# Modulation products on a 32-column stationary block spread over the four column quarters of TensorE

## The chip, the cores and the metric

The kernel runs on one core of a Trainium2 chip. The metric is the device time of one execution in microseconds (us); the median of three runs is given. In the profile PE is TensorE's matmul, PEld its weight load, DVE VectorE, ACT ScalarE, POOL GpSimd, SP the engine that issues most DMAs.

## What is computed

Two layers of a block with attention, retention and state-space heads and an MLP, all in float32. Ahead of both sub-layers of a layer stands a modulation, which is what the change touches:

```python
sc = jax.nn.silu(c); scc = jax.nn.silu(c_ctx)          # two vectors of 1024
mod   = sc  @ w_mod[layer] + b_mod[layer]              # [1024] @ [1024, 6144]
mod_c = scc @ w_mod[layer] + b_mod[layer]              # the same for the context stream
sh1, sc1, g1, sh2, sc2, g2 = jnp.split(mod, 6, axis=-1)
h  = rmsnorm(x, norm_g[0]) * (1 + sc1) + sh1           # ahead of the mixers
x  = x + g1 * rmsnorm(o, norm_g[1])                    # behind them
```

So each layer has two vector-by-matrix products with a matrix of 1024 x 6144, which is 25 MB a layer in float32.

## The kernel before

The 6144 columns are worked in 12 sections of 512 columns (`sec`), the 1024 rows in 8 chunks of 128 (`k`). For a section on TensorE the stationary operand is `csil[:, k, :]`, 128 rows by 2 columns (the two streams), the moving operand is a chunk of weights, 128x512, and the output is a tile `mq` of 2x512 in PSUM, summed over the chunks. ACT copies it to SBUF as `mr`; four transposes turn it into columns, one feature to a partition (`mps`), DVE adds the bias (`mc`) and writes the table `abc` from which the norm is modulated.

The 12 sections of layer 0 are made in three places. At the program's start, in `start`, sections 0, 2 and 3 are made by `mod_exact` on TensorE, with weights in tiles `m`, and section 1 by `mod_sums`, in which DVE multiplies and adds eight chunks for two streams into `acc_m` and TensorE only sums over the partitions (L369). Woven into them are the transposes of the normed input (`xps`) and their copies back to SBUF. The first weights of the mixers, `kv`, are converted there too (`wr_kv` to `wh_kv` and `wl_kv`). The next norm needs sections 0 and 2 for its first four chunks, and sections 1 and 3 for the others; then come the `kvp` products. In the mixers of layer 0, sections 4 to 9 are a list of steps (`mods_gen`) that runs in the gaps of attention and retention. Sections 4 and 5 go through `mod_split`: ACT rounds the raw weights `wr_m` to a high part `wh_m`, POOL subtracts for the low part `wl_m`, and `chl`, four columns of high and low parts of `csil`, is multiplied with either. Sections 6 to 9 go through `mod_whole`: float32 products straight from `wr_m`. Sections 10, 11 and all of layer 1 are made later by `mod_groups`, outside the change.

All raw weights in the mixers share the tag `wr` with three buffers of 128x1024, so a load waits until the buffer three loads earlier has been read. Nearly all DMAs are issued by SP, in order. The order on each engine comes from a scheduler that keeps the program's order as priority and moves instructions by its own estimates, so an edit in one place reorders its neighbours. Instructions on one engine run in that order. Behind section 9 follow the retention heads 1 to 3 (`dTkr`, `dTqr`, `rs`, `rd`, the state `rst`, the output `ry`), then the output projection (`op`).

Of the kernel before, what the change touches and what calls it, by code (L numbers as in the profile page):

```python
# [20 lines left out]
D = 1024  # L21
# [21 lines left out]
def shape_constants():  # L43
# [16 lines left out]
    # query minus key in a chunk; steps from the chunk before to a query, for both directions  # L60
# [20 lines left out]
def tile_hybrid_backbone(  # L81
# [87 lines left out]
    def rsqrt_mean(y, ssum, use, D=D, n=1):  # L169
        """1 / sqrt(ssum / D + EPS): the scalar engine's root, then one Newton step on its reciprocal"""  # L170
# [12 lines left out]
    def softplus(y, xin, n):  # L183
        """log(1 + exp(x)) = max(x, 0) + 2 atanh(e / (2 + e)), e = exp(-|x|)"""
# [17 lines left out]
    def wraw(src, shape, name):  # L202
        """one half of a unit: at most 1024 elements a partition"""
        r = wp.tile([128, 1024], F32, tag="wr", name=f"wr_{name}", bufs=3)
        v = r[:, : shape[1] * shape[2]].rearrange("p (a b) -> p a b", a=shape[1])
        for s_ap, c0, n0 in src:
            nc.sync.dma_start(v[:, :, c0 : c0 + n0], s_ap)
        return v

    def wunit(src, shape, name, lo_eng=None, pool=None):  # L210
        """src: function (first row block, row blocks) -> list of (AP, first column, columns)"""
# [13 lines left out]
    def wcols(w, k0, cols):  # L225
        """row blocks from k0 on; cols: list of (column in w, column in the unit, columns)"""
# [18 lines left out]
    chl = cp.tile([128, KC, 4], F32R, name="chl")  # L245
    V.tensor_copy(chl[:, :, 0:4:2], csil)
    V.tensor_tensor(chl[:, :, 1:4:2], csil, chl[:, :, 0:4:2].bitcast(F32), ALU.subtract)

    # gate * norm gain: [mixer or channel, stream]
    grow = [dp.tile([2, 2, D], F32, name=f"grow{l}") for l in range(DEPTH)]  # L250
    pcol = [cp.tile([128, R_END], F32, name=f"pcol{l}") for l in range(DEPTH)]
    # per layer: A1, B1, A2, B2, each [chunk, stream]
# [18 lines left out]
    def mod_cols(l, sec, q, nrow):  # L271
        """section of 512 columns of the modulation, as per-feature columns; q: [nrow, 512] in SBUF"""
        which = sec // 2
        k0 = 4 * (sec % 2)
        if q.shape[0] == 128:
            o = q
        else:
            o = pC([128, 4, nrow], f"mps{l}_{sec}")
            for k in range(4):
                transpose(o[:, k, :], q[:, k * 128 : (k + 1) * 128])  # L280
# [4 lines left out]
        if nrow == 2:  # L285
            V.tensor_tensor(tk, o, bcol, ALU.add)
        else:
            u = sm.tile([128, 4, 4], F32, tag="mc_u", name=f"mu{l}_{sec}")
            S.activation(u, o, AF.Copy)
            V.tensor_tensor(tk, u[:, :, 0:4:2], u[:, :, 1:4:2], ALU.add)  # L290
            V.tensor_tensor(tk, tk, bcol, ALU.add)
# [28 lines left out]
    def mod_whole(l, sec, row):  # L320
        q = pB([2, 512], f"mq{l}_{sec}")
        for u in range(4):
            r = wraw(wcols(w_mod[l], 0, [(sec * 512, 0, 512)])(2 * u, 2), (128, 2, 512), f"m{l}_{sec}_{u}")
            for k in range(2):
                T.matmul(q, csil[:, 2 * u + k, :], r[:, k], start=u + k == 0, stop=u + k == 4)
            if u == 3:
                r = row([2, 512], f"mr{l}_{sec}")
# [4 lines left out]
    def mod_split(l, sec, row):  # L332
        q = pB([4, 512], f"mq{l}_{sec}")
        for u in range(4):
            if u % 2 == 0:
                hu, lu = wunit(wcols(w_mod[l], 2 * u, [(sec * 512, 0, 512)]), (128, 4, 512), f"m{l}_{sec}_{u}", G)
            h, lo = hu[:, 2 * (u % 2) : 2 * (u % 2) + 2], lu[:, 2 * (u % 2) : 2 * (u % 2) + 2]
            for k in range(2):
                for w in (h, lo):
# [1134 lines left out]
```

## Time and profile before

| what | value |
|---|---|
| median of 3 runs | 1888.09 us (1886.2 to 1888.5) |
| span of the profiled execution | 1880.8 us |
| median less that span | 7.3 us |
| PE busy | 1753.1 us, 93% |
| DVE, ACT, POOL busy | 1219.7, 703.0, 369.1 us |
| granted TensorE clock, mean | 0.972 |

The profile gives the span from the first to the last instruction; its execution has no other time of its own, and the runs beside it take 7.3 us more than the span. A float32 matmul stands in the trace as two records of PE, each with a weight load of its own; one of the rounded type stands as one record. PE records overlap, since a record lasts until its last result is written: what a record costs in a row of them is the distance between starts.

### The profile page before, as it was taken

What the parts mean: (1) busy time and instruction counts of PE and PEld (TensorE: products, weight loads), DVE (VectorE), ACT (ScalarE), POOL (GpSimd) and SP (SyncE); (2) the same over time, 40 slices, a digit from 0 to 9 for tenths busy, and PEclk for the clock granted to TensorE, in tenths of its full rate; (3) what the DMA queues carried; (4) which work ended last, traced back from release to release, by engine and by line L of the source; (5) the groups of instructions that cost most, each with busy time, mean ns of one, the idle gap of its engine ahead of it and who ended that gap; (6) DMA issues with size and microseconds to landing.
All of it is one profiled execution on the core that took longest, in us unless ns stands there. A gap on an engine that the chain in (4) does not pass through costs nothing. (4 is left out here: it accounts for less than half of the span.)

```text
span 1880.8 us, 24641 instructions
## 1 busy us (share of the span) xinstructions
PE 1753.1 (93%) x8991; PEld 1443.0 (77%) x8991; DVE 1219.7 (65%) x2462; ACT 703.0 (37%) x1267; POOL 369.1 (20%) x391
## 2 busy tenths in 40 slices
PE   6987999997999999999999979888987999999998
PEld 2877977655878888888888868777866788888886
DVE  5868985664668566566566586788876654444445
ACT  5543376652461111201201275433772532222222
POOL 0047232313001100100100132553022021111112
PEclk9999999997999999999999999999996999999999
DMA  8410243366444334434434433224324432222332
GB/s 274 124 52 32 89 149 104 104 182 184 146 135 136 124 101 132 125 107 123 126 105 118 152 123 91 65 71 124 100 73 110 147 122 90 90 90 91 102 105 95
DMA packets 189078, 217.00 MB, mean 115 GB/s; under 512 B 67667, under 2 KB 142237, under 8 KB 188957
## 3 DMA queue, kind: packets, MB, share of 16 engines
q1 hardware_dynamic: 188956, 215.43, 37.8%
q8 instruction: 71, 1.16, 0.2%
q14 instruction: 51, 0.41, 0.1%
HBM read 189.66 MB, written 25.72 MB: 115 GB/s over the span
## 5 line engine op out<-in xcount | busy, mean ns | idle before, releaser
L467 PE MATMUL f<-h_h,wh_f 128*128 128x512 f32 (+1 forms) x800 | 280.3, 351 | 1.4 <-ACT h_h L448 1.4
L469 PE MATMUL f<-h_h,wl_f 128*128 128x512 f32 (+1 forms) x800 | 281.0, 352 | 0.0
L468 PE MATMUL f<-h_l,wh_f 128*128 128x512 f32 (+1 forms) x800 | 280.1, 350 | 0.8 <-DVE h_l L449 0.8
L1299 POOL TENSOR_TENSOR r<-r 128x768 f32<-128x768 f32 (+1 forms) x64 | 93.8, 1466 | 847.4 <-ACT r L1298 837.8
L467 PE MATMUL f<-wh_g,uh 128*128 128x512 f32 x640 | 253.0, 396 | 4.1 <-DVE acc L1327 1.7
L468 PE MATMUL f<-wl_g,uh 128*128 128x512 f32 x640 | 252.6, 395 | 0.0
L469 PE MATMUL f<-wh_g,ul 128*128 128x512 f32 x640 | 251.8, 394 | 0.0
L221 ACT ACTIVATE wh_f<-wr_f 128x1024 fp32r<-128x1024 f32 x64 | 66.5, 1055 | 377.2 <-PE f L469 164.4
L1329 DVE TENSOR_TENSOR acc<-acc,f 128x512 f32<-128x512 f32 x140 | 96.0, 686 | 121.0 <-PE f L469 119.6
L467 PEld LDWEIGHTS f<-h_h,wh_f 128*128 128x128 f32 x800 | 152.0, 190 | 23.0 <-ACT h_h L448 1.5
L468 PEld LDWEIGHTS f<-h_l,wh_f 128*128 128x128 f32 x800 | 151.1, 189 | 22.8 <-DVE h_l L449 1.0
L469 PEld LDWEIGHTS f<-h_h,wl_f 128*128 128x128 f32 x800 | 151.2, 189 | 20.8
L405 DVE SCALAR_TENSOR_TENSOR ga<-wr_mg,cg_a,ga 128x512 f32<-128x512 f32 x216 | 153.6, 762 | 14.6 <-DMA wr_mg<-in_w_mod_dram 14.6
L467 PEld LDWEIGHTS f<-wh_g,uh 128*128 128x128 f32 x640 | 120.1, 188 | 33.5 <-DVE acc L1327 2.2
L469 PEld LDWEIGHTS f<-wh_g,ul 128*128 128x128 f32 x640 | 120.1, 188 | 28.8
L468 PEld LDWEIGHTS f<-wl_g,uh 128*128 128x128 f32 x640 | 120.2, 188 | 27.4 <-DVE wl_g L222 0.2
L1298 ACT ACTIVATE r<-f 128x768 f32<-128x768 f32 (+1 forms) x64 | 44.8, 699 | 193.4 <-PE f L469 133.4
L1300 DVE CAST uh<-r 128x768 fp32r<-128x768 f32 (+1 forms) x64 | 32.3, 505 | 123.2 <-POOL r L1299 123.2
L222 DVE TENSOR_TENSOR wl_f<-wr_f,wh_f 128x1024 fp32r<-128x1024 f32 x64 | 77.6, 1220 | 51.3 <-ACT wh_f L221 51.3
L222 DVE TENSOR_TENSOR wl_g<-wr_g,wh_g 128x1024 fp32r<-128x1024 f32 x62 | 76.6, 1241 | 50.9 <-ACT wh_g L221 50.8
L221 ACT ACTIVATE wh_g<-wr_g 128x1024 fp32r<-128x1024 f32 x64 | 67.3, 1056 | 94.2 <-DMA wr_g<-in_w_ff_dram 53.6
L467 PE MATMUL xbc<-h_h,wh_xbc 128*128 128x512 f32 (+1 forms) x208 | 73.5, 353 | 7.7 <-ACT cin L692 7.7
(405 smaller groups left out, 3774.3 us busy)
## 6 DMA issues: line engine op xcount, KB each, us to landing
wr_f<-in_w_ff_dram SPq DMA_DIRECT2D x64, 512.0 KB, 3.7
wr_g<-in_w_ff_dram SPq DMA_DIRECT2D x64, 512.0 KB, 3.5
wr_mg<-in_w_mod_dram SPq DMA_DIRECT2D x192, 128.0 KB, 2.9
wr_m<-in_w_mod_dram SPq DMA_DIRECT2D x24, 512.0 KB, 3.8
m<-in_w_mod_dram SPq DMA_DIRECT2D x32, 256.0 KB, 4.2
wr_o<-in_w_out_dram SPq DMA_DIRECT2D x16, 512.0 KB, 4.1
wr_xbc<-in_w_in_dram SPq DMA_DIRECT2D x14, 512.0 KB, 5.3
xmid<-xt SPq DMA_DIRECT2D x10, 512.0 KB, 2.6
```

Of the source, the lines that this page charges most:

```text
L221: S.activation(hv[:, a0 : a0 + an], r, AF.Copy)
L222: (lo_eng or V).tensor_tensor(lv[:, a0 : a0 + an], r, hv[:, a0 : a0 + an].bitcast(F32), ALU.subtract)
L405: V.scalar_tensor_tensor(acc[:, s], r2[:, k % 2], w, acc[:, s], ALU.mult, ALU.add)
L467: T.matmul(o, a[0], b[0], start=first, stop=False)
L468: T.matmul(o, a[0], b[1], start=False, stop=False)
L469: T.matmul(o, a[1], b[0], start=False, stop=last)
L1298: S.activation(r, q[:, :NT], AF.Relu)
L1299: G.tensor_tensor(r, r, r, ALU.mult)
L1300: V.tensor_copy(uh, r)
L1329: V.tensor_tensor(acc[tt][:, ns], acc[tt][:, ns], qs[tt][half], ALU.add)
```

## The change

The stationary operand becomes `cwide[:, k, :]`: the two columns of `csil` and 30 columns of zeros. Chunk `k` writes to partitions 32 (k mod 4) to 32 (k mod 4) + 31 of a 128x512 tile `mq`, so two chunks share each quarter and successive chunks go to different quarters. The built program has a column position of 0, 32, 64 or 96 at these matmuls, and a tile of 128x32 both before and after. The four partial sums are added in the step that made the four transposes: `mr` (now 128x512) is the stationary operand of four float32 matmuls with `qsum`, 128x2, whose ones sit where a row's number modulo 32 is the stream's. `mod_split` is gone: sections 4 and 5 go through `mod_whole`. `mod_sums`, with `csil`, stays. The parts of the diff that are left out drop comments.

```diff
-    chl = cp.tile([128, KC, 4], F32R, name="chl")
-    V.tensor_copy(chl[:, :, 0:4:2], csil)
-    V.tensor_tensor(chl[:, :, 1:4:2], csil, chl[:, :, 0:4:2].bitcast(F32), ALU.subtract)
+    cwide = cp.tile([128, KC, 32], F32, name="cwide")
+    G.memset(cwide, 0.0)
+    G.tensor_copy(cwide[:, :, 0:2], csil)
+    qsum = cp.tile([128, 2], F32, name="qsum")
+    V.tensor_reduce(qsum, ident.rearrange("p (j r) -> p r j", r=32)[:, 0:2, :], AX.X, ALU.add)
...
     def mod_cols(l, sec, q, nrow):
-        if q.shape[0] == 128:
+        if len(q.shape) == 3:
             o = q
         else:
             o = pC([128, 4, nrow], f"mps{l}_{sec}")
             for k in range(4):
-                transpose(o[:, k, :], q[:, k * 128 : (k + 1) * 128])
+                T.matmul(o[:, k, :], q[:, k * 128 : (k + 1) * 128], qsum, start=True, stop=True)
...
+    def mod_quarter(q, k, v):
+        j = k % 4
+        T.matmul(q[32 * j : 32 * j + 32], cwide[:, k, :], v, start=k < 4, stop=k >= KC - 4)
+
     def mod_exact(l, sec, raw, row):
-        q = pB([2, 512], f"mq{l}_{sec}")
+        q = pB([128, 512], f"mq{l}_{sec}")
         for k in range(KC):
...
-            T.matmul(q, csil[:, k, :], v, start=k == 0, stop=k == KC - 1)
+            mod_quarter(q, k, v)
...
     def mod_whole(l, sec, row):
-        q = pB([2, 512], f"mq{l}_{sec}")
+        q = pB([128, 512], f"mq{l}_{sec}")
...
             for k in range(2):
-                T.matmul(q, csil[:, 2 * u + k, :], r[:, k], start=u + k == 0, stop=u + k == 4)
+                mod_quarter(q, 2 * u + k, r[:, k])
...
-    def mod_split(l, sec, row):
...
-                    yield from (mod_whole if s in (6,7,8,9,) else mod_split)(0, s, lambda shape, name: mp.tile([128, 512], F32, tag="fcol", name=name)[: shape[0]])
+                    yield from mod_whole(0, s, lambda shape, name: mp.tile([128, 512], F32, tag="fcol", name=name)[: shape[0]])
```

The scheduler's order moves with it. In the start stage DVE had these rows before; names read as tile, section, chunk and buffer, so `acc_m<-m_1_0` is the first chunk of section 1:

```order
L269 TENSOR_SCALAR pcol_104<-pcol_104 128x42
L361 TENSOR_SCALAR acc_m<-m_1_0_225,csil 128x512 x2
L286 TENSOR_TENSOR mc_0_218<-mps_0_213,pcol_104 128x4x2
L295 COPY abc_106<-mc_0_218 128x8
L1411 COPY x_120<-xps_200 128x512
L363 SCALAR_TENSOR_TENSOR acc_m<-m_1_1_232,csil,acc_m 128x512 x2
L363 SCALAR_TENSOR_TENSOR acc_m<-m_1_2_250,csil,acc_m 128x512 x2
```

And now:

```order
L273 TENSOR_SCALAR pcol_106<-pcol_106 128x42
L1398 COPY x_122<-xps_202 128x512
L289 TENSOR_TENSOR mc_0_220<-mps_0_215,pcol_106 128x4x2
L348 TENSOR_SCALAR acc_m<-m_1_0_227,csil 128x512
L293 COPY abc_108<-mc_0_220 128x8
L348 TENSOR_SCALAR acc_m<-m_1_0_227,csil 128x512
L1398 COPY x_122<-xps_238 128x512
L350 SCALAR_TENSOR_TENSOR acc_m<-m_1_1_234,csil,acc_m 128x512 x2
```

The first sums of section 1 now stand behind `mc_0`, which needs the end of section 0, and one copy of `xps` stands ahead of both. On PE, at the same place, the products of section 0 stood together before:

```order
L152 MATMUL pps_178<-ident,prow_172 128x125
L314 MATMUL mq_0_165<-m_0_2_182,csil 2x512
L314 MATMUL mq_0_165<-m_0_3_185,csil 2x512
L314 MATMUL mq_0_165<-m_0_4_188,csil 2x512
L314 MATMUL mq_0_165<-m_0_5_191,csil 2x512
L314 MATMUL mq_0_165<-m_0_6_194,csil 2x512
L314 MATMUL mq_0_165<-m_0_7_197,csil 2x512
L152 MATMUL xps_200<-ident,x_120 128x128 x8
L152 MATMUL mps_0_213<-ident,mr_0_211 128x2 x4
L314 MATMUL mq_2_221<-m_2_0_222,csil 2x512
```

Now sixteen transposes `xps` stand between them:

```order
L152 MATMUL xps_202<-ident,x_122 128x128 x6
L310 MATMUL mq_0_167<-m_0_2_184,cwide 32x512
L152 MATMUL xps_202<-ident,x_122 128x128 x2
L152 MATMUL xps_238<-ident,x_122 128x128 x3
L310 MATMUL mq_0_167<-m_0_3_187,cwide 32x512
L152 MATMUL xps_238<-ident,x_122 128x128 x5
L310 MATMUL mq_0_167<-m_0_4_190,cwide 32x512
L310 MATMUL mq_0_167<-m_0_5_193,cwide 32x512
L310 MATMUL mq_0_167<-m_0_6_196,cwide 32x512
L310 MATMUL mq_0_167<-m_0_7_199,cwide 32x512
L310 MATMUL mq_2_223<-m_2_0_224,cwide 32x512
L284 MATMUL mps_0_215<-qsum,mr_0_213 128x2 x4
```

The last six chunks of section 0 are no longer one block, and the sum over quarters, `mps_0`, comes behind the first chunk of section 2.

In attention PE had, at the seam of sections 4 and 5, pairs of products with a high and a low part between score products `s` and transposes `pt`:

```order
L340 MATMUL mq_4_3652<-wh_m_4_2_3774,chl 4x512
L340 MATMUL mq_4_3652<-wl_m_4_2_3775,chl 4x512
L340 MATMUL mq_5_3948<-wh_m_5_0_3949,chl 4x512
L340 MATMUL mq_5_3948<-wl_m_5_0_3950,chl 4x512
L152 MATMUL pt_3600<-ident,P_3595 128x128 x3
L152 MATMUL pt_3606<-ident,P_3595 128x128 x3
L938 MATMUL s_3692<-k1a_2958,qha_3293 128x512
L939 MATMUL s_3692<-k1a_2958,qla_3294 128x512
L938 MATMUL s_3692<-k1a_2958,qha_3293 128x256
L939 MATMUL s_3692<-k1a_2958,qla_3294 128x256
L340 MATMUL mq_5_3948<-wh_m_5_0_3949,chl 4x512
L340 MATMUL mq_5_3948<-wl_m_5_0_3950,chl 4x512
```

There stands now this, in which `x2` is two chunks of one buffer:

```order
L310 MATMUL mq_4_3654<-wr_m_4_3_3842,cwide 32x512 x2
L152 MATMUL pt_3602<-ident,P_3597 128x128 x3
L152 MATMUL pt_3608<-ident,P_3597 128x128 x3
L925 MATMUL s_3684<-k1a_2960,qha_3295 128x512
L926 MATMUL s_3684<-k1a_2960,qla_3296 128x512
L925 MATMUL s_3684<-k1a_2960,qha_3295 128x256
L926 MATMUL s_3684<-k1a_2960,qla_3296 128x256
L310 MATMUL mq_5_3927<-wr_m_5_0_3928,cwide 32x512 x2
L152 MATMUL pt_3625<-ident,P_3620 128x128 x3
L152 MATMUL pt_3631<-ident,P_3620 128x128 x3
L310 MATMUL mq_5_3927<-wr_m_5_1_3970,cwide 32x512 x2
L925 MATMUL s_3729<-k1a_2960,qha_3295 128x256
```

The work between keeps its order; the products of a section come in groups of two chunks, here and there more.

In SP's queue, in retention, the last load of section 7 stood ahead of the store of section 5's gate (`grow_5`) before:

```order
L207 DMA wr_m_7_3_4196<-in_w_mod_dram 128x2x512
L1083 DMA gb_4202<-in_ret_gn_g_dram 128x64
L1083 DMA gb_4202<-in_ret_gn_b_dram 128x64
L307 DMA grow_102<-grow_5_4128 4x128 x2
L1085 DMA ry_4040<-sgd_496 128x6x64
L207 DMA wr_m_8_0_4222<-in_w_mod_dram 128x2x512
```

Now the load `wr_m_7_3` stands behind `grow_5`:

```order
L305 DMA grow_104<-grow_5_4084 4x128 x2
L207 DMA wr_m_7_3_4152<-in_w_mod_dram 128x2x512
L1070 DMA gb_4158<-in_ret_gn_g_dram 128x64
L1070 DMA gb_4158<-in_ret_gn_b_dram 128x64
L1072 DMA ry_4009<-sgd_498 128x6x64
L207 DMA wr_m_8_0_4178<-in_w_mod_dram 128x2x512
```

That load has moved past one store, which waits for ACT's copy of section 5's gate.

Further on in SP's queue the next head's keys `ddkr` stood among the loads of section 9 before:

```order
L207 DMA wr_m_9_0_4249<-in_w_mod_dram 128x2x512
L207 DMA wr_m_9_1_4268<-in_w_mod_dram 128x2x512
L1004 DMA ddkr_4322<-krd_494 128x6x64
L207 DMA wr_m_9_2_4272<-in_w_mod_dram 128x2x512
L207 DMA wr_m_9_3_4276<-in_w_mod_dram 128x2x512
L1004 DMA ddkr_4322<-krd_494 128x6x64
L1004 DMA ddqr_4323<-qrd_493 128x6x64 x2
```

Now all of `ddkr` stands behind section 9:

```order
L207 DMA wr_m_9_1_4224<-in_w_mod_dram 128x2x512
L207 DMA wr_m_9_2_4228<-in_w_mod_dram 128x2x512
L207 DMA wr_m_9_3_4232<-in_w_mod_dram 128x2x512
L991 DMA ddkr_4278<-krd_496 128x6x64 x2
L991 DMA ddqr_4279<-qrd_495 128x6x64 x2
```

One of the two loads of `ddkr` has moved past two loads of section 9.

## Rows read from the trace of the kernel before

**Rows 1.** The profile page, head and part 1: busy us (share) xinstructions.

```profile
span 1880.8 us, 24641 instructions
...
PE 1753.1 (93%) x8991; PEld 1443.0 (77%) x8991; DVE 1219.7 (65%) x2462; ACT 703.0 (37%) x1267; POOL 369.1 (20%) x391
```

**Rows 2.** Busy time by stretch: us, then each engine, PEclk, DMA share, GB/s.

```profile
355.00:417.00 62.00, 58.11 (x316) 33.52 (x314) 44.59 (x110) 38.27 (x80) 15.26 (x8) 1.00 0.59 164
417.00:436.00 19.00, 16.45 (x49) 3.66 (x49) 6.59 (x22) 2.46 (x6) 3.55 (x5) 1.00 0.92 267
436.00:468.00 32.00, 22.41 (x131) 20.63 (x130) 19.55 (x50) 10.15 (x15) 13.14 (x13) 0.68 0.58 172
```

**Rows 3.** Instructions of tile mq: duration ns min/median/max, first and last start.

```profile
L325 PE MATMUL mq<-wr_m,csil x64: 590/592/593, 368.9 to 435.3; 128*2 128x512 f32 x64
```

**Rows 4.** Timeline of PE, 17 to 38 us: start us, us, operation, count.

```profile
17.39 5.31 PE L314 MATMUL mq<-m,csil 128*2 128x512 f32 x12
22.64 1.09 PE L152 MATMUL xps<-ident,x 128*128 128x128 f32 x8
...
37.08 1.84 PE L369 MATMUL mq<-sel,acc_m 128*128 128x1 f32 x16
```

**Rows 5.** Timeline of PE, 355 to 434 us.

```profile
355.18 0.40 PE L340 MATMUL mq<-wh_m,chl 128*4 128x512 f32 x1
355.41 0.39 PE L340 MATMUL mq<-wl_m,chl 128*4 128x512 f32 x1
...
394.92 0.41 PE L152 MATMUL mps<-ident,mr 4*128 4x4 f32 x4
...
433.96 1.88 PE L325 MATMUL mq<-wr_m,csil 128*2 128x512 f32 x4 [0.23 <-DMA wr_m<-in_w_mod_dram]
```

**Rows 6.** Groups by line and shape: busy us, mean ns of one.

```profile
L222 POOL TENSOR_TENSOR wl_m<-wr_m,wh_m 128x1024 fp32r<-128x1024 f32 x8 | 19.3, 2420 | 37.8 <-ACT wh_m L221 37.8
...
L221 ACT ACTIVATE wh_m<-wr_m 128x1024 fp32r<-128x1024 f32 x8 | 8.4, 1056 | 3.9 <-DMA wr_m<-in_w_mod_dram 2.8 <-PE s L939 1.1
```

**Rows 7.** Instructions of tile mx, 340 to 400 us: duration ns min/median/max.

```profile
L943 DVE TENSOR_TENSOR mx<-mx,qrs x16: 140/156/1394, 341.2 to 391.3; 128x1 f32<-128x1 f32 x16
```

**Rows 8.** Timeline of DVE in the start stage.

```profile
23.20 0.88 DVE L361 TENSOR_SCALAR acc_m<-m,csil 128x512 f32<-128x512 f32 x2
...
34.14 2.73 DVE L363 SCALAR_TENSOR_TENSOR acc_m<-m,csil,acc_m 128x512 f32<-128x512 f32 x4
...
39.59 0.16 DVE L297 SCALAR_TENSOR_TENSOR abc<-mc,pcol 128x8 f32<-128x8 f32 x1
```

**Rows 9.** Timeline of ACT in the start stage.

```profile
22.93 0.57 ACT L317 ACTIVATE mr<-mq 2x512 f32<-2x512 f32 x1
...
37.78 1.63 ACT L221 ACTIVATE wh_kv<-wr_kv 128x804 fp32r<-128x804 f32 x2
39.84 0.88 ACT L443 ACTIVATE x<-x,abc 128x128 f32<-128x128 f32 x2 [0.44 <-DVE mc L286]
...
48.28 0.57 ACT L317 ACTIVATE mr<-mq 2x512 f32<-2x512 f32 x1
```

**Rows 10.** Timeline of SP's DMA issues, 406 to 413 us.

```profile
406.43 0.84 SPq L207 DMA_DIRECT2D wr_m<-in_w_mod_dram  x1
...
412.26 0.60 SPq L307 DMA_DIRECT2D grow<-grow  x2
```

**Rows 11.** DMA issues between 413 and 436 us: count, KB each, us to landing.

```profile
wr_m<-in_w_mod_dram SPq DMA_DIRECT2D x8, 512.0 KB, 3.6
```

**Rows 12.** Waits of PE, 330 to 470 us: us in total, times, longest us.

```profile
PE ry L1057 <- DVE rst L1052: 8.7, 2, 6.2
PE mq L325 <- DMA wr_m<-in_w_mod_dram: 2.1, 4, 1.1
```

**Rows 13.** Timeline of DVE, 442 to 461 us.

```profile
442.63 1.02 DVE L1105 SCALAR_TENSOR_TENSOR mix_l<-sT,pcol,mix_h 128x768 fp32r<-128x768 f32 x1 [0.50 <-ACT mix_h L1101]
...
459.49 1.22 DVE L222 TENSOR_TENSOR wl_o<-wr_o,wh_o 128x1024 fp32r<-128x1024 f32 x1
```

More of the change, by code (lines that the diff above doesn't have):

```diff
@@ L284, in mod_cols @@
         bcol = bc(pcol[l][:, boff : boff + 4], 2, 2)
[L285 to L291, printed above, removed]
+        V.tensor_tensor(tk, o, bcol, ALU.add)
         g0 = R_G + {0: 0, 1: 0, 2: 8, 3: 0, 4: 16, 5: 24}[which] + k0
@@ L313, in mod_exact @@
             nc.sync.dma_start(v, w_mod[l, k * 128 : (k + 1) * 128, sec * 512 : (sec + 1) * 512])
-            T.matmul(q, csil[:, k, :], v, start=k == 0, stop=k == KC - 1)
+            mod_quarter(q, k, v)
             yield
-        r = row([2, 512], f"mr{l}_{sec}")
+        r = row([128, 512], f"mr{l}_{sec}")
         S.activation(r, q, AF.Copy)
@@ L324, in mod_whole @@
             for k in range(2):
-                T.matmul(q, csil[:, 2 * u + k, :], r[:, k], start=u + k == 0, stop=u + k == 4)
+                mod_quarter(q, 2 * u + k, r[:, k])
             if u == 3:
-                r = row([2, 512], f"mr{l}_{sec}")
+                r = row([128, 512], f"mr{l}_{sec}")
                 S.activation(r, q, AF.Copy)
@@ L330, in mod_whole @@
         mod_cols(l, sec, r, 2)
-    def mod_split(l, sec, row):
[L333 to L339, printed above, removed]
-                    T.matmul(q, chl[:, 2 * u + k, :], w[:, k, :], start=(u == 0 and k == 0 and w is h),
-                             stop=(u == 3 and k == 1 and w is lo))
-            if u == 3:
-                r = row([4, 512], f"mr{l}_{sec}")
-                S.activation(r, q, AF.Copy)
-            yield
-        mod_cols(l, sec, r, 4)
     def mod_sums(l, sec, acc, raw=None):
```

## The prediction, made before the changed kernel ran

> **What bounds the kernel now.** I read the page first, then busy time by stretch, then the modulation's own tile, then the timelines around it. PE is busy 93% of the span [rows 1], so a product taken off PE is worth its full length wherever PE is the last to finish, and nothing where DVE, ACT or a DMA is. The products that the change touches lie in two parts of layer 0, 13 to 49 us and 355 to 436 us. In the second they cross three regimes [rows 2]: until 417 us PE is busy 58.1 of 62 us; from 417 to 436 us the DMAs are busy 92% of the time at 267 GB/s; from 436 to 468 us PE is busy 22.4 of 32 us, the granted clock has fallen to 0.68, and the retention heads run as a chain, with PE waiting 8.7 us for DVE's states `rst` [rows 12]. Behind that the output projection fills PE, so I take a shift at 468 us to be a shift of the end.
>
> **The price of a chunk.** Twelve float32 records in a row take 5.31 us and the last one 0.59, so starts lie (5.31 - 0.59) / 11 = 0.429 us apart [rows 3, 4]; a chunk is two records, 0.86 us. Of the split kind, two records start 0.23 us apart and a chunk is 0.46 us [rows 5]. Before, sections 4 to 7 cost, up to 417 us, 32 x 0.23 + 32 x 0.429 = 21.1 us of PE; now they are 32 float32 chunks, 64 records.
>
> No row shows two records on different column quarters; all products before are on the first. I bound it from both sides. *No overlap*: 64 x 0.429 = 27.5 us, a loss of 6.4. *Full overlap*, four chunks in the time of one: in the new order the 32 chunks stand in runs of 6, 2, 2, 2, 1, 5, 3, 3, 1, 5 and 2, hence 4+2+2+2+2+4+2+2+2+4+2 = 28 slots of 0.429, 12.0 us, a gain of 9.1. *Half overlap*: records start in order, and the second record of a chunk needs the quarter of its first, so it waits 0.429 us; but the next chunk's first record can start beside it. A run of n chunks then takes n + 1 slots: 43 slots, 18.4 us, a gain of 2.7. I take the half overlap, because the pair of records per chunk on one quarter is what the trace shows and what the change keeps.
>
> The Trainium skill, page "TensorE: Matmul & The Clock Gate", section "Part 3: Packing small matmuls — row/col tiling", says that products whose outputs lie in different groups of 32 PSUM partitions run side by side (2.38x for three), and that matmuls start and end strictly in order. By that factor alone the 64 records would take about 27.5 / 2.38 = 11.6 us, an estimate from the page; by its order rule, a chunk's second record holds the queue and the 18.4 us stay. No row of the kernel before shows either.
>
> **The sum over quarters.** Four transposes took 0.41 us [rows 5]. Now they are four float32 products with a 128x128 stationary operand, two records each. The nearest row is the sum over partitions of section 1, 16 records of that shape in 1.84 us, with the last 0.25: 0.106 apart [rows 4]. Eight take 7 x 0.106 + 0.25 = 0.99 us, +0.58 a section; three such until 417 us make +1.7. So PE gains 2.7 - 1.7 = 1.0 us there.
>
> **What the split no longer costs.** ACT loses 8 x 1.056 = 8.4 us and POOL 8 x 2.42 = 19.3 us [rows 6]. ACT was busy 38.3 of 62 us where PE was busy 58.1 [rows 2], so PE covers it; without that cover it would be worth up to PE's idle time there, 62 - 58.1 = 3.9 us. Some of it may count: the smallest DVE instruction of the softmax, `mx`, takes 156 ns in the median and 1394 ns at most [rows 7], and POOL, at work beside it, is a possible cause that no row proves. I take 1.0 us, bounds 0 and 3.9. The copy of `mr` grows from 2 to 128 partitions with the same 512 columns; it stays at 0.57 us [rows 9].
>
> **The start.** On PE sixteen transposes, 2 x 1.09 us [rows 4], now stand ahead of the end of section 0, while its last six chunks need 2 + 2 + 5 = 9 slots in place of 12 (-1.3): `mq_0` ends 0.9 us later, and the dearer sum (+0.6) brings `mc_0` some 1.4 us later, at about 25.5 us. DVE's first sum of section 1 started at 23.20 and did not wait for `mc_0` [rows 8]; now it does: 2.3 us late. One copy, about as long as a sum (2.73 / 4 = 0.68), leaves that chain, so it ends at 38.5 in place of 36.87 us. The table entry of section 2 (39.59) now stands behind that of section 1, hence behind the 1.84 us of its sum on PE: ACT's first modulation starts near 40.7 in place of 39.84 us, and the second `wh_kv` conversion, 1.63 / 2 = 0.82 us, which was hidden ahead of it [rows 9], follows it. ACT's copy of section 3 comes 1.7 us late (48.28 before), and with the dearer sum the second half of the norm 2.3 us late. Behind these PE queues the `kvp` products. I take +2.3 us. Below, -1 if PE's queue catches up in the `kvp` products; above, +4 if they also wait at section 3's sum.
>
> **The DMA-bound stretch.** Sections 8 and 9 are 16 chunks in runs of 8, 2 and 6: 19 slots in place of 32, 5.6 us less PE. But a load is 512 KB [rows 11], 1.96 us at 267 GB/s, against 1.72 us for its two chunks before; so most of it turns into waiting for DMA, which took only 2.1 us before [rows 12]. Against it, `wr_m_7_3`, issued at 406.43 ahead of the store of `grow_5` at 412.26 [rows 10], now follows that store, and its 1.96 us fall into this stretch; for it, `ddkr` leaves the loads of section 9. Earlier release of the three buffers is worth about (1.72 - 1.29) / 3 = 0.14 us a load. I take -1.0, bounds -4 and +2.
>
> **The tail.** DVE's `mix_l`, 1.02 us amid the states of head 1, now comes behind them, and one of the `wl_o` conversions of 1.22 us leaves the chain of head 2 [rows 13], but the first `wr_o` loads are issued later. I take -1.3, bounds -3 and +3. Work on `cwide` and `qsum` takes the place of that on `chl` on engines that wait for the first weights: nothing, and if that cover were gone a few instructions of about 0.2 us.
>
> **Sum.** -1.0 - 1.0 + 2.3 - 1.0 - 1.3 = -2.0 us on a span of 1880.8. What lies around the span, 7.3 us to the median of 1888.09, stays: 1886.1 us. The likeliest case's own range is 1880 to 1891.
>
> **Rivals.** A measurement of this kernel can tell about 0.2%, 3.8 us, from no change.
>
> *Full overlap.* The Trainium skill, page "TensorEngine Tiling (Array Packing)", section "Theoretical Speedup", gives up to 4x for a dimension of at most 32. In rows of this case: -9.1 + 1.7 = -7.4 until 417 us, -1.0 for the split, +1.9 at the start (one slot less), -1.5 with the DMAs, -1.3 in the tail: -9.3, 1878.8 us. For it, the four positions are really set; against it, two records a chunk on one quarter.
>
> *No overlap: slower.* Records on different quarters still start 0.429 us apart, because a moving operand of 128 partitions takes the whole input. Then +6.4 + 1.7 = +8.1, -1.0 for the split, +3.6 at the start, 0 with the DMAs, -1.3: +9.4, 1897.5 us. It decides where two neighbouring chunks take 4 slots and not 3.
>
> *The gain does not pass on.* In attention products of the modulation fill gaps while PE would wait for the softmax; if PE's saved time turns into such waits, the gains of 1.0 and 1.0 vanish, the start costs its +4 and the rest nets out: 1892 us.
>
> **How the numbers follow.** Half overlap 0.45 (faster 0.17, same 0.23, slower 0.05), full overlap 0.22 (faster), no overlap 0.18 (slower 0.17, same 0.01), gain not passed on 0.15 (same 0.08, slower 0.07). Faster 0.39, same 0.32, slower 0.29. The range 1876 to 1896 takes in the first, second and last case and leaves out most of no overlap: about 0.18.
>
> **What would show it.** In the timeline of PE, neighbouring chunks of `mq`: 3 slots for two and 5 for four confirm the half overlap. `acc_m` starting at 25 us or later and ACT's copy of section 3 near 50 us confirm the start. PE waits for `wr_m` of more than 2.1 us between 412 and 434 us confirm the DMA bound. The prediction is wrong if `mq` overlaps fully or not at all, or if the order in the tail moves the output projection by more than 3 us.

## The result: 0.5% slower, and the profile after

The changed kernel took 1897.67 us in the median (4 runs, 1895.64 to 1900.16), the kernel before 1888.3 beside it: a ratio of 1.0052 [1.0036, 1.0068]. In a later batch it was 1897.91 (12 runs) against 1891.37 (35 runs), 1.0030 [1.0011, 1.0049]. The prediction was 1886.1 us with a range to 1896: the sign and the range both missed.

```profile
span 1898.4 us, 24691 instructions
...
PE 1753.8 (92%) x9027; PEld 1460.9 (77%) x9027; DVE 1220.9 (64%) x2459; ACT 695.1 (37%) x1257; POOL 352.0 (19%) x385
```

This head of the page after answers to [rows 1]. The spans differ by 17.6 us, the medians by 9.4: the execution of before that was profiled first lies some 6 us under its median, that of the change 2.5 us above. A run takes only about 1.8 us more than its own span, so the 7.3 us that I put around the span were for the most part this one fast execution. So both were profiled once more (`e15`, `e16`), and where sizes matter I compare those two (9.8 us apart). Starts and ends of PE's instructions cut the span into stretches; the last stretch ends with PE's last instruction, some 9.5 us ahead of the span's end:

| stretch (us) | before, first profile | before again | after | after again |
|---|---|---|---|---|
| S: start, to the last `kvp` | 66.3 | 66.2 | 71.3 | 68.7 |
| A: to the last `dTqa` (layer 0's projections) | 290.1 | 290.3 | 292.2 | 291.4 |
| B: attention, to the first `rs` | 47.4 | 47.5 | 44.5 | 45.6 |
| C: to section 9's sum `mps`, granted clock | 32.7, 1.00 | 36.7, 0.86 | 42.1, 0.64 | 41.5, 0.63 |
| D: to the output projection | 31.9, 0.68 | 33.2, 0.64 | 34.1, 0.70 | 34.4, 0.70 |
| E: output projection | 77.2 | 77.2 | 79.6 | 79.7 |
| F: the rest | 1326.0 | 1325.7 | 1325.0 | 1325.0 |

Attention won 1.9 us (last pair of profiles); the start lost 2.5, the rest of A 1.1, C lost 4.8, D 1.2, E 2.5.

The timeline of PE after (start, us, engine, line, operation, count, idle time before with its releaser) shows what a chunk costs, to be read against [rows 3 to 5]:

```profile
364.15 1.91 PE L310 MATMUL mq<-wr_m,cwide 128*32 128x512 f32 x12
...
408.04 1.60 PE L1022 MATMUL rs<-qT,kT 64*128 64x128 f32 x12
412.10 2.79 PE L1026 MATMUL rd<-vrr,W 128*128 128x64 f32 x12 [2.46 <-DVE vrr L1082]
...
418.92 1.87 PE L284 MATMUL mps<-qsum,mr 128*128 128x2 f32 x8 [0.51 <-ACT grow L302]
...
438.37 1.36 PE L310 MATMUL mq<-wr_m,cwide 128*32 128x512 f32 x4 [2.54 <-DMA wr_m<-in_w_mod_dram]
...
445.60 1.14 PE L310 MATMUL mq<-wr_m,cwide 128*32 128x512 f32 x8
448.34 1.05 PE L310 MATMUL mq<-wr_m,cwide 128*32 128x512 f32 x4 [1.60 <-DMA wr_m<-in_w_mod_dram]
450.15 1.05 PE L284 MATMUL mps<-qsum,mr 128*128 128x2 f32 x8 [0.76 <-ACT mr L331]
```

Two chunks (x4) take 1.05 us, four (x8) 1.14, six (x12) 1.91, where twelve records took 5.31 [rows 4]. But `rd` at 412.10 took 2.79 us for what lasts 1.52 at the full clock: the clock had fallen to the lower of its levels, 1.2 GHz. Busy time by stretch, beside [rows 2]:

```profile
355.00:417.00 62.00, 53.69 (x317) 36.72 (x316) 39.45 (x100) 34.47 (x79) 3.21 (x2) 0.96 0.59 170
417.00:436.00 19.00, 17.56 (x74) 12.44 (x72) 8.15 (x24) 4.43 (x9) 2.28 (x4) 0.51 0.44 131
436.00:468.00 32.00, 24.24 (x134) 18.24 (x134) 15.96 (x44) 7.27 (x11) 6.80 (x7) 0.76 0.76 196
```

The stretch that was bound by the DMAs is not any more: 131 GB/s where it was 267, and a granted clock of 0.51 where it was 1.00. (The same work stands 4.2 us later here: the first `rs` starts at 408.04 us, before's at 403.87.) PE is busy there for 17.56 us against 16.45, since its transposes and `ry` products run at half speed too.

### The profile page after: what moved, and what is told of

Its sections match the earlier page's. It is cut to its first block, busy times and chain, and to the rows that moved or that the text cites. A ratio compares the mean times of both kernels' runs of the same rounds, so it can differ in the third digit from the quotient of the medians.

```text
span 1898.4 us, 24691 instructions
## 1 busy us (share of the span) xinstructions
PE 1753.8 (92%) x9027; PEld 1460.9 (77%) x9027; DVE 1220.9 (64%) x2459; ACT 695.1 (37%) x1257; POOL 352.0 (19%) x385
## 3 DMA queue, kind: packets, MB, share of 16 engines
q1 hardware_dynamic: 188956, 215.43, 38.2%
## 5 line engine op out<-in xcount | busy, mean ns | idle before, releaser
L221 ACT ACTIVATE wh_f<-wr_f 128x1024 fp32r<-128x1024 f32 x64 | 66.5, 1055 | 376.2 <-PE f L456 136.7
L454 PEld LDWEIGHTS f<-wh_g,uh 128*128 128x128 f32 x640 | 120.3, 188 | 33.4 <-DVE acc L1314 2.5
L1285 ACT ACTIVATE r<-f 128x768 f32<-128x768 f32 (+1 forms) x64 | 44.7, 699 | 193.2 <-PE f L456 133.3
L221 ACT ACTIVATE wh_g<-wr_g 128x1024 fp32r<-128x1024 f32 x64 | 67.3, 1055 | 92.5 <-DMA wr_g<-in_w_ff_dram 51.1
```

The costliest lines, as they stand in the source:

```text
L221: S.activation(hv[:, a0 : a0 + an], r, AF.Copy)
L454: T.matmul(o, a[0], b[0], start=first, stop=False)
L1285: S.activation(r, q[:, :NT], AF.Relu)
```

## The experiments

Ratios are to the kernel before, run beside each on the same chip (medians of before, in the order of the five batches: 1889.82, 1888.94, 1888.22, 1891.37, 1889.21). C is with its granted clock.

| run | median us (runs) | ratio [95%] | S | B | C | D | E |
|---|---|---|---|---|---|---|---|
| e1, e6 (one kernel) | 1891.23 (12), 1885.87 (5) | 1.0016 [1.0000, 1.0031], 0.9981 [0.9957, 1.0006] | 65.8, 66.9 | 44.3, 47.1 | 36.2 at 0.76, 37.6 at 0.73 | 38.5, 32.0 | 79.6, 78.5 |
| e2 | 1892.39 (12) | 1.0008 [0.9994, 1.0021] | 69.7 | 47.6 | 32.4 at 1.00 | 32.2 | 78.3 |
| e3 | 1898.88 (5) | 1.0055 [1.0043, 1.0067] | 65.8 | 51.5 | 40.7 at 0.86 | 33.4 | 77.2 |
| e4 | 1897.4 (6) | 1.0039 [1.0023, 1.0054] | 67.6 | 51.8 | 41.5 at 0.88 | 31.8 | 78.3 |
| e5 | 1893.69 (11) | 1.0025 [1.0007, 1.0043] | 70.3 | 44.6 | 38.3 at 0.69 | 34.2 | 78.0 |
| e7 | 1899.03 (11) | 1.0041 [1.0020, 1.0061] | 69.4 | 49.9 | 35.5 at 0.81 | 36.9 | 79.7 |
| e8 | 1895.35 (11) | 1.0038 [1.0014, 1.0062] | 70.9 | 47.1 | 36.9 at 0.77 | 29.8 | 78.5 |
| e9 | 1885.27 (12) | 0.9982 [0.9969, 0.9995] | 66.5 | 44.4 | 36.9 at 0.96 | 32.6 | 78.2 |
| e10 | 1903.68 (6) | 1.0078 [1.0057, 1.0099] | 71.3 | 44.2 | 35.4 at 0.95 | 38.8 | 82.3 |
| e11 | 1892.73 (12) | 1.0020 [1.0001, 1.0039] | 66.7 | 45.3 | 40.0 at 0.66 | 39.9 | 77.8 |
| e12 | 1883.87 (12) | 0.9977 [0.9963, 0.9991] | 67.3 | 44.5 | 38.2 at 0.87 | 33.1 | 78.2 |
| e13 | 1890.08 (12) | 0.9988 [0.9972, 1.0004] | 71.4 | 45.3 | 36.6 at 0.91 | 33.3 | 77.2 |
| e14 | 1886.78 (12) | 0.9984 [0.9967, 1.0000] | 68.1 | 47.4 | 34.8 at 1.00 | 33.6 | 78.5 |
| e15, before | 1891.94 (12) | 1.0008 [0.9994, 1.0022] | 66.2 | 47.5 | 36.7 at 0.86 | 33.2 | 77.2 |
| e16, after | 1897.91 (12) | 1.0030 [1.0011, 1.0049] | 68.7 | 45.6 | 41.5 at 0.63 | 34.4 | 79.7 |
| e17 | 1903.1 (6) | 1.0069 [1.0043, 1.0094] | 70.8 | 47.2 | 39.8 at 0.61 | 40.7 | 78.1 |
| e18 | 1895.3 (12) | 1.0025 [1.0001, 1.0050] | 66.1 | 44.5 | 40.1 at 0.59 | 36.0 | 78.0 |

The two runs of one kernel, e1 and e6, differ by 0.35%: between occasions some 3 us either way must be allowed beyond the intervals, so only larger differences, or those of one batch, carry a verdict. A stretch is of one execution and says less than a median.

**The parts of the change: e1 to e4.** e1 is the change with sections 0, 2 and 3 left as before:

```
-        q = pB([128, 512], f"mq{l}_{sec}")
+        q = pB([2, 512], f"mq{l}_{sec}")
...
-            mod_quarter(q, k, v)
+            T.matmul(q, csil[:, k, :], v, start=k == 0, stop=k == KC - 1)
...
```

> The kernel after, with sections 0, 2 and 3 of the start made as before (two columns, one quarter, transposes); quarters in sections 4 to 9 alone. Theory A (the order around the products, not the products): the start costs nothing (the kvp products start near 43.4 us as before, dTqa ends near 356), the attention stretch gives back 3 to 4 us, and what is lost is lost between 405 and 470 us; the time falls by about 5 us against the kernel after, to some 1889 to 1893 us. Theory B (each section pays for the 32-column block and for the sum over the quarters, about 1 us with its wait for mr, wherever it stands): six sections still pay, the time falls by about 3 us only, to 1894 or 1895. Theory C (the loss is that of the retention stretch alone): 1897, unchanged, because a shift in the start is hidden later.

e2 is the kernel before with quarters in those three sections alone (the same lines the other way).

> The kernel before, with quarters in sections 0, 2 and 3 of the start alone; sections 4 to 9 as before, the split with them. Theory A: the kvp products end about 5 us later than in the kernel before and the shift stays to the end: 1892 to 1894 us. Theory B: three sections pay about 1 us each, 1891. Theory C: 1888, no change.

e3 is the kernel before with sections 4 and 5 by `mod_whole`, two columns, no split:

```
-yield from (mod_whole if s in (6,7,8,9,) else mod_split)(0, s, ...)
+yield from mod_whole(0, s, ...)
```

> The kernel before with sections 4 and 5 not split: float32 products of two columns on one quarter, start and sections 6 to 9 as before. 16 chunks cost 0.86 us of PE in place of 0.46 (+6.4 us in the attention stretch), and ACT and POOL lose their conversions. Theory A: the attention stretch becomes 2 to 6 us longer and nothing else changes, 1890 to 1894 us. Rival: the split's conversions on ACT and POOL were what attention waited for, and the time stays or falls, 1885 to 1888. If, without any quarters, the stretch of the retention gets longer as in the kernel after, its order (the loads of section 7 and later behind the store of grow) comes from the missing split and not from the quarters.

e4 is the change with every chunk on the first quarter, 32 columns wide:

```
-        T.matmul(q[32 * j : 32 * j + 32], cwide[:, k, :], v, start=k < 4, stop=k >= KC - 4)
+        T.matmul(q, cwide[:, k, :], v, start=k == 0, stop=k == KC - 1)
...
```

The sum then takes 32 rows of `qsum` in place of 128.

> The kernel after with all chunks on the first quarter: 32-column stationary block, output of 32 partitions, sum with qsum over 32 rows. Nothing can overlap; a chunk costs two records 0.43 us apart. Theory A: PE loses 0.43 x 2 us for each chunk that lay beside another, some 15 us of PE in sections 4 to 7, of which the attention stretch passes on 4 to 9; order as in the kernel after: 1900 to 1906 us. Rival (the overlap is worth nothing to the end, the 32 columns and the sum are what costs): within 2 us of the kernel after, 1896 to 1899.

Eight records on one quarter, in the timeline of PE of e4:

```profile
428.73 3.62 PE L309 MATMUL mq<-wr_m,cwide 128*32 128x512 f32 x8
```

Against 1.14 us on four quarters that is 3.2 times. In attention the overlap is worth 6 to 7 us (B 51.8 against 44.5 and 45.6), and e3, which has none either, has e4's B. Yet e4 and the change take the same time. In C, e4 has 40.1 us of PE work at a clock of 0.88 and takes 41.5 us; the change has 32.8 us of it at 0.64 and takes 42.1; D and E are longer by 2.3 and 1.3 us. Where the clock stays up, the sum over the quarters is not the loss either: e4 has it in all nine sections and is not slower than e3, which has transposes (1.0039 [1.0023, 1.0054] against 1.0055 [1.0043, 1.0067], one batch). e3 loses some 10 us where 2 to 6 were expected: the split without quarters is worth that much. e2 costs about 1.5 us by its ratio, less than the 3.5 us by which its S is longer than before's.

**What hangs on the stores, the split and POOL: e5 to e8.** e5 issues the store of `grow_5` behind the last load of section 9 in SP's queue, and not ahead of the fourth load of section 7:

```
+            if (l, sec) == (0, 5):
+                late.append(store)
...
+                for f in late:
+                    f()
```

> The kernel after with one thing moved: the store of grow_5 is issued behind the last load of section 9 in place of ahead of the fourth load of section 7; the order of loads, products and of ACT and POOL is as in the kernel after up to that point. Theory D (late loads): in the kernel after SP stood at that store from about 410 to 419 us, nine loads of 512 KB came late, the last products of section 9 were done near 449.4 us against 435.8 before, and the heads of the retention and the output projection, which stand behind them on PE, went with them. Then the last products come 6 to 9 us earlier, and so do op and the end: 1889 to 1892 us. Theory E (the sums over the quarters at half clock with their waits for mr, and the lower granted clock of 417 to 436 us, make the loss): the last products move by under 2 us, 1896 to 1898.

e6 is the kernel of e1 once more, on another occasion; in spite of its name no store is moved in it.

> The kernel of e1 a second time, on another occasion, as the base of the next two (start as before, quarters in sections 4 to 9): 1889 to 1893 us if its time is that of the first occasion; a difference of more than 3 us would say how far runs of different occasions can be compared.

e7 is the kernel before with quarters in sections 6 to 9 alone: the split of 4 and 5 and the start are as before.

> The kernel before with quarters in sections 6 to 9 alone; the start, and the split of sections 4 and 5, as before. Theory D with the split as the cause of the late loads (ACT and POOL read the raw weights as soon as they land, so the buffers come free and the fourth load of section 7 is issued ahead of the store of grow_5): the retention stretch loses nothing against the kernel before, sections 6 and 7 give 1 to 3 us back in attention, 1884 to 1888 us. Theory E: sections 7, 8 and 9 pay for their sums in the retention stretch as in the kernel after: 1893 to 1896.

e8 is the change with the `mix_l` of layer 0's attention on DVE (`put(j, f[:, :NT], None, G if l else V)`).

> The kernel after with the low parts of the three attention tiles of layer 0 (mix_l from fa, 128x768, 1.80 us each on POOL) made by DVE (0.96 us each). In the kernel after DVE's small operations ahead of the states of head 2 ended 0.02 us behind the ends of POOL's operations five times in a row (1.45, 1.38, 1.73, 0.89 and 0.78 us in place of 0.17). Theory F (DVE's small operations stand still while POOL works, and two of POOL's five operations there are these parts): the wait of PE for the states of head 2 falls from 9.3 to 6 or 7 us, the time by 2 to 3 us, 1894 to 1896. Rival: the DVE time added, 3 x 0.96 us, takes its place in the same chain; within 1 us of the kernel after.

e5 lies 1 to 5 us under the change by its ratio, within what occasions differ by, and its clock in C is 0.69, low all the same. e7 keeps the split and the old start and is as slow as the change, so the loss comes from neither: quarters in 6 to 9 alone cost 0.41%, 7.7 us. (Its S of 69.4 us, with the old start, shows how far S varies from one execution to the next.) In e8 PE's longest wait for `rst` fell from 9.34 to 6.3 us and D from 34.1 to 29.8 us, but its time cannot be told from the change's.

**Quarters only where PE is the bound: e9 to e12.** e9 leaves the start and sections 7 to 9 as before (two columns, transposes), quarters in 4 to 6 alone:

```
+                    yield from (mod_whole if s < 7 else mod_plain)(0, s, ...)
```

> Start as before, quarters in sections 4 to 6 (attention), sections 7 to 9 as before (two columns, one quarter, transposes). Theory G (the products that overlap leave PE idle beside the loads, the granted clock falls to half from some 410 us on, and all the other work of PE in the retention runs at half speed): the clock from the first rs to the sum of section 9 is 1.00 again, this stretch takes 32 us as in the kernel before in place of 36 to 42, and the 3 us won in attention stay: 1882 to 1887 us. Theory D (late loads and the order of the stores alone, whatever the clock): the stretch gains only what the order gives, 3 us or so, 1888 to 1892.

e10 is the change with each product of sections 7 to 9 doubled by one with a stationary block of zeros on the same quarter, which adds nothing to the sums but 24 chunks of PE work:

```
+                if sec in (7, 8, 9):
+                    T.matmul(q[32 * (kk % 4) : 32 * (kk % 4) + 32], czero, r[:, k], start=False, stop=False)
```

> The kernel after with more work: in sections 7 to 9 each product is doubled by one with a stationary block of zeros on the same quarter, which adds nothing to the sum; 24 chunks, 0.43 us or more each, 10 to 20 us of PE in all. Theory G: the granted clock from the first rs to the sum of section 9 rises from 0.63 to 0.9 or more, and the kernel is no slower than the kernel after in spite of the work, 1888 to 1897 us. Theory D or E (PE's work or the loads, not the clock): the added products lengthen the chain by 5 us or more, 1902 or above.

e11 is e1 with the late store of e5, and e12 is e9 with it.

> The kernel of e1 (start as before, quarters in 4 to 9) with the store of grow_5 moved behind the last load as in e5. If the late store and the start add up, it is 3 to 5 us below e1 on the same chip, 1884 to 1888 us; if the clock decides (theory G), the stretch from the first rs to the sum of section 9 still takes 35 us or more at a granted clock under 0.85 and the time stays within 2 us of e1, 1888 to 1892.

> The kernel of e9 with the store of grow_5 behind the loads: sections 8 and 9 may come up to 5 us earlier. Theory G: as e9 or up to 3 us below it, 1880 to 1886 us, if the clock stays at 1.00 in that stretch; no gain over e9 if the products and the DMAs set the stretch anyway.

e11 and e12 stood on one chip and differ in sections 7 to 9 alone: 1892.73 against 1883.87 us, with intervals apart. Quarters there cost 8.9 us, although they take less of PE. The median granted clock of the whole run is 0.960 in e11 and 0.968 in e12. Busy time over C, first of e9, then of e10 (C, D, E), then of the change:

```profile
400.70:437.60 36.90, 32.53 (x146) 14.69 (x145) 18.68 (x55) 7.11 (x12) 5.32 (x6) 0.96 0.79 219
```

```profile
408.90:444.30 35.40, 30.46 (x194) 17.02 (x190) 19.20 (x55) 7.81 (x13) 5.94 (x6) 0.95 0.85 234
444.30:483.10 38.80, 29.33 (x134) 27.11 (x135) 23.37 (x56) 10.87 (x15) 13.06 (x12) 0.53 0.47 140
483.10:565.40 82.30, 82.27 (x376) 67.01 (x374) 49.33 (x124) 39.54 (x78) 0.00 (x0) 0.93 0.36 124
```

```profile
408.00:450.20 42.20, 32.83 (x143) 22.44 (x142) 18.60 (x55) 6.93 (x12) 4.03 (x5) 0.64 0.64 176
```

The zero products bring C from 42.1 to 35.4 us: PE is given more to do, is granted 0.95 instead of 0.64, and is done with all of it sooner. But the clock falls later instead, in D (0.53), and the whole is 0.78% slower than before; that they would cost nothing over all was wrong.

**What separates the start from the tail, and both kernels again: e13 to e16.** e13 is e9 with quarters in the start too, so it differs from the change in sections 7 to 9 alone. e14 has quarters in 4 and 5 alone.

> The kernel of e9 with quarters in sections 0, 2 and 3 of the start too; it differs from the kernel after only in sections 7 to 9. If the start costs what e2 shows against the kernel before (1.5 us, -1 to 4), 1886 to 1889 us; if it costs what the kernel after shows against e1 (about 6 us), 1890 to 1893 us.

> Start as before, quarters in sections 4 and 5 alone, in place of the split; 6 to 9 as before. Against e9, eight chunks of section 6 lose their overlap, some 1.5 to 3 us of PE in attention. If attention passes it on, 1886 to 1889 us; if the loads of section 9 set the end of the stretch behind it, as e9's row of the last product (435.6 us, 435.8 before) suggests, the same as e9, 1884 to 1887.

> The kernel before, for a second profile: the first has a span of 1880.8 us where the median run has some 1886.5. Theory G expects the granted clock at 1.00 again from the first rs to the sum of section 9, 31 to 34 us; the 6 us lie elsewhere. If that stretch varies by more than 4 us from one execution to the next, the profiles of single executions can't carry the account of the retention.

> The kernel after, for a second profile and a ratio on the same chip as e9's kind: 1.004 to 1.006 of the kernel before again. Theory G: clock of 0.6 to 0.75 and 38 to 43 us from the first rs to the sum of section 9, against 1.00 and 31 to 34 us in the kernel before.

e13 and the change (e16), one batch, take 1890.08 and 1897.91: 7.8 us for sections 7 to 9. e13 less e9 is 0.0006 of 1890, 1.1 us for the start; with quarters in 7 to 9 beside it the start costs 7.8 us by e17 less e18 (one batch, below) and 0.9 by e5 less e11, so its price is not settled. e14 and e9 take the same time, so section 6 on quarters brings nothing that can be told. e14 and e3 differ only in the overlap in sections 4 and 5: 0.9984 against 1.0055, 13 us of the end, of which B has 4.1 us and C 5.9 in their profiles, so a gain in attention can be passed on. Busy time over C, of before in its first profile and again, and of the change again:

```profile
403.87:436.58 32.71, 28.96 (x134) 12.59 (x134) 17.54 (x56) 6.83 (x13) 5.21 (x6) 1.00 0.86 240
```

```profile
403.90:440.60 36.70, 33.57 (x134) 15.77 (x133) 17.70 (x56) 6.82 (x13) 5.21 (x6) 0.86 0.78 214
```

```profile
405.70:447.20 41.50, 32.82 (x143) 22.44 (x142) 18.56 (x55) 6.93 (x12) 4.09 (x6) 0.63 0.65 179
```

The kernel before, too, can lose its clock in C: 1.00 in its first profile, 0.86 here. The same 134 records of PE are busy for 28.96 us there and 33.57 here; C is 4.0 us longer and D 1.3, about all of the 5.2 us between the two spans. Here the program is the same and its clock is not. Over the 35 runs of before in this batch the time falls by 1.08 us for each 0.001 of mean granted clock (least squares, r = -0.69); the median clock is 0.967 before and 0.960 after, worth 7 x 1.08 = 7.6 us, an estimate, where the medians differ by 6.5. The same estimate for e11 and e12, 8 x 1.08 = 8.6 us, stands beside their 8.9. Over the 12 runs of the change the slope is 1.38 us (r = -0.88); its one run at 0.967 took 1884.39 us. Such a slope does not say whether the clock or the waiting comes first.

**Is the wait ahead of `rd` the trigger? e17 and e18.** The last full-speed products of the change before the fall are `rs`; behind them PE waits 2.46 us for `vrr`, whose load follows the store of `grow_4` on SP. e17 puts that store, and that of `grow_5`, behind later loads; e18 is e17 with the old start.

> The kernel after with both stores moved on SP's queue: that of grow_4 behind the load of vrr, that of grow_5 behind the last load of section 9 (as in e5). In the kernel after the first rd waited 2.46 us for DVE's vrr, because the scheduler put DVE's mu and vrr behind W, and the clock fell at that rd (2.79 us in place of 1.52); here mu and the first vrr stand ahead of the second W, as in the kernel before. If this wait starts the fall: rd without a wait and at full clock, 1.00 for some us more, 33 to 37 us from the first rs to the sum of section 9 in place of 42, 1886 to 1891 us. If the clock falls anyway, a few us later, because PE has too little to do there: clock under 0.8, 36 to 39 us, 1890 to 1895, as e5.

> The same two moves on the kernel of e1 (start as before, quarters in 4 to 9). If the wait ahead of rd starts the fall, this is the best of all: the 3 us of attention, no loss in the retention, 1881 to 1885 us, not above e9. If the clock falls anyway, 1887 to 1892 us, above e9.

```profile
415.28 2.59 PE L1036 MATMUL rd<-vrr,W 128*128 128x64 f32 x12 [1.80 <-DVE vrr L1092]
```

The wait shrank to 1.80 us in e17 (1.40 in e18) and the clock fell all the same, to 0.61 and 0.59 over C; both kernels are slower than either expectation had them. So that one wait is not shown to be the trigger, and what exactly makes the clock fall at this place stays open.

## Why the prediction was wrong

**The price of a chunk.** "I take the half overlap" failed: a chunk's second record does not hold up the next chunk, four chunks take 1.14 us where half overlap gives 5 slots, 4 x 0.429 + 0.59 = 2.3. The trace agrees with the speed-up of up to 4 that the Trainium skill gives in its page "TensorEngine Tiling (Array Packing)", section "Theoretical Speedup": 3.2 times here. The rival of full overlap had the mechanism right and the time wrong, 1878.8 us. The rival of no overlap had the time, 1897.5 us, by luck: these rows refute its mechanism.

**Attention.** -1.0 on PE and -1.0 for the split made -2.0; B fell by 1.9 to 2.9 us. Right in size, but not by its terms: with full overlap PE's part would have been -7.4. PE's busy time over B did fall, from 44.7 us (both profiles of before) to 38.7 and 40.2; part of it became waiting. That POOL's split had slowed the softmax is borne out. The row of [rows 7] now has no long instruction:

```profile
L930 DVE TENSOR_TENSOR mx<-mx,qrs x17: 146/158/160, 340.4 to 395.3; 128x1 f32<-128x1 f32 x17
```

And before, the long ones each end 0.01 us behind one of POOL's `wl_m` (timelines of DVE, then of POOL, of before):

```profile
361.87 0.96 DVE L943 TENSOR_TENSOR mx<-mx,qrs 128x1 f32<-128x1 f32 x1
364.57 1.39 DVE L943 TENSOR_TENSOR mx<-mx,qrs 128x1 f32<-128x1 f32 x1
```

```profile
360.42 2.39 POOL L222 TENSOR_TENSOR wl_m<-wr_m,wh_m 128x1024 fp32r<-128x1024 f32 x1 [0.27 <-ACT wh_m L221]
363.56 2.39 POOL L222 TENSOR_TENSOR wl_m<-wr_m,wh_m 128x1024 fp32r<-128x1024 f32 x1 [0.75 <-ACT wh_m L221]
```

What is won against the split passes on where sections 7 to 9 stay as they were: e9, with B 3.1 us shorter than in before again, takes 3.4 us less by its ratio. Its last products of section 9 start at 433.68 us behind a wait of 2.48 us for their load, those of before at 433.96 [rows 5] and, again, at 438.00. The rival "the gain does not pass on" is not borne out in attention; in the change the gain was lost behind it. (Its 1892 us is the start's +4 alone; the -2.3 us of the other terms were dropped without a reason.)

**The sum over quarters.** 0.99 us forecast; 0.95 to 1.05 measured at the full clock, 1.87 at half. Ahead of four of them PE waits 0.5 to 0.8 us for a copy by ACT, which the sum lacked.

**The start.** +2.3, bounds -1 and +4: S grew by 2.5 (again) and 5.0 us (first pair); of it 1.1 to 1.5 us reach the end by e13 and e2, more by e17 and e18. S alone goes from 65.8 to 69.4 us in kernels with the old start, so the sizes are rough. The cause was as told: DVE's first sum of section 1 waits for `mc_0`. It starts at 25.55 us in the second profile of the change, where about 25.5 was forecast, and at 27.18 in the first. The timeline of DVE in the first, to be read against [rows 8]:

```profile
27.10 0.17 DVE L289 TENSOR_TENSOR mc<-mps,pcol 128x8 f32<-128x8 f32 x1 [2.74 <-PE mps L284]
27.18 0.48 DVE L348 TENSOR_SCALAR acc_m<-m,csil 128x512 f32<-128x512 f32 x1
```

**The DMA-bound stretch and the tail: the step that decided.** "I take -1.0, bounds -4 and +2" and "I take -1.3, bounds -3 and +3" came out as +4.8 (C) and +3.7 (D and E). I took products off PE in a stretch where DMAs bound it and held that this could cost little but waiting for the DMAs, with the clock as it was. The clock fell: C's granted clock went from 0.86 to 0.63 (last pair), and PE was busy for 32.8 us in C, hardly less than before's 33.6, though its products had become cheaper. And the waits grew: PE idles for 8.7 us of C where it idled for 3.1, of it 2.5 for `vrr`, 3.4 for `wr_m` and 2.8 for ACT's copies ahead of the sums. The waits for `wr_m` that I named as the sign of the DMA bound did not come between 412 and 434 us. In the first profile they end at 438.37 (2.54 us) and 448.34 (1.60 us): the loads were late first, at 129 GB/s, and then the DMAs were busy 0.83 of the time, at 257. Busy time of the change in the window that I named and from the start of the first of these waits to the end of the second:

```profile
412.00:434.00 22.00, 20.63 (x91) 17.20 (x93) 10.82 (x29) 4.84 (x9) 3.45 (x5) 0.50 0.44 129
435.83:448.34 12.51, 7.62 (x33) 3.46 (x31) 4.65 (x18) 1.50 (x2) 0.00 (x0) 0.73 0.83 257
```

The timeline of SP's DMA issues:

```profile
409.84 0.57 SPq L1103 DMA_DIRECT2D fr<-ssdd  x1
418.89 0.60 SPq L305 DMA_DIRECT2D grow<-grow  x2
419.92 0.40 SPq L207 DMA_DIRECT2D wr_m<-in_w_mod_dram  x1
```

SP issues nothing for 9 us: the store of `grow_5` waits for its section's sum on a slow PE, and the load stands behind it. That order alone is worth a few us at most (e5; e12 against e9 and e11 against e1 show none). In E the first `op` products wait 1.5 us for DVE's `wl_o` (second profile of the change; none in before again), and six behind them take 0.63 us each, where they take 0.39 at the full clock; the tail had no term for this.

That quarters in sections 7 to 9 (6 to 9 in e7) cost 7.7 to 8.9 us is shown by three comparisons, each in one batch (e11 and e12, e13 and e16, e7 and before). That the clock costs time in C is shown by the two profiles of before and by e10, where more work on PE made C shorter, though not the whole. How the loss divides between the clock and the waits is not shown. The Trainium skill, page "TensorE: Matmul & The Clock Gate", section "HAM oscillation — how this bites in real kernels", describes thin products that wait for DMA and drop to half the clock; the trace agrees in kind, with `rd` at 2.79 us for 1.52 in a stretch with 8.7 us of waits, but which wait starts the fall is not shown. The prediction drew on that page for the order of matmuls alone and gave the clock no rival.

**The sum by medians.** Quarters in place of the split -3 (e9, e14), the start +1.1 to +1.5, sections 7 to 9 +7.7 to +8.9: +5.8 to +7.4, where 6.5 and 9.4 were measured. (e9, e13 and e16 are links of one chain and add up by themselves; e2, e7, e11 and e12 are the test.) The better version leaves sections 7 to 9 and the start as they were: e12, 0.9977 [0.9963, 0.9991], and e9, 0.9982 [0.9969, 0.9995], lie below both kernels, and so does e14 on another chip. Against before that is 3 to 4 us, no more than occasions differ by.

## What to carry to other kernels

Pack small products on column quarters where PE is the last to finish, and try leaving them unpacked where PE waits for loads: here the saved time became idle time, and all other work on PE paid when the clock fell. Before costing a change by durations at the full clock, look at the granted clock of the stretch in more than one execution; if it moves from run to run (1.00 and 0.86 here), a loss of the clock is a rival with a price: at most the PE time of that stretch once more.

## What the runs showed of the hardware

- Float32 products on different column quarters overlap fully although each is two records: 5.31 to 1.91 us for six chunks, 3.62 to 1.14 for four.
- The clock of one program falls in some executions at places where it stays up in others. In both profiles of before PE waits 1.09 us for a copy at the same place. In the first the `dTqr` behind it takes 0.82 us, in the second 1.30:

```profile
410.14 0.43 PE L1056 MATMUL ry<-vrr,W 128*128 128x64 f32 x2 [1.09 <-ACT mr L328]
410.41 0.82 PE L152 MATMUL dTqr<-ident,ddqr 128*128 128x128 f32 x6
```

```profile
410.22 0.43 PE L1056 MATMUL ry<-vrr,W 128*128 128x64 f32 x2 [1.09 <-ACT mr L328]
410.50 1.30 PE L152 MATMUL dTqr<-ident,ddqr 128*128 128x128 f32 x6
```

- Small DVE instructions stretch beside POOL, as `mx` did above. These take about 0.17 us elsewhere; here, each ends 0.02 us behind one of POOL's (timelines of DVE, then of POOL, of the change):

```profile
465.31 1.45 DVE L159 TENSOR_SCALAR grs<-rq_t 128x6 int32<-128x6 int32 x1
466.79 1.38 DVE L165 TENSOR_TENSOR rq_t<-grs 128x6 f32<-128x6 f32 x1
468.21 1.73 DVE L166 TENSOR_TENSOR rq_t<-rq_t,rq_h 128x6 f32<-128x6 f32 x1
```

```profile
464.93 1.81 POOL L1090 TENSOR_TENSOR mix_l<-fa,mix_h 128x768 fp32r<-128x768 f32 x1
466.69 1.46 POOL L993 TENSOR_TENSOR W<-ddkr,kwt 128x768 f32<-128x768 f32 x1
468.12 1.80 POOL L1090 TENSOR_TENSOR mix_l<-fa,mix_h 128x768 fp32r<-128x768 f32 x1
```

The Trainium skill, page "SBUF — State Buffer", section "SBUF: two separate sides", says that GpSimd and VectorE share a pair of ports and that one waits out the other's whole instruction, for VectorE instructions in a two-port mode or with two inputs from SBUF; the ends agree. These instructions lie in the chain of states that D waits for (9.34 us ahead of `ry`), and that wait is 3 us shorter in the profile of e8.
